# A hybrid decoder layer: the forget gate's logarithm taken straight from the tanh, its complement moved to ACT

## The chip, the cores and the metric

The kernel runs on one core of a Trainium2 chip. The metric is the device time of one execution in microseconds (us). A core has TensorE (PE in the profile, its weight loads PEld), VectorE (DVE), ScalarE (ACT), GpSimd (POOL) and SyncE (SP), whose queue issues the DMA transfers. Each engine works off its own list of instructions in order; engines wait for each other by semaphores. Matmul results land in PSUM banks, everything else lies in SBUF, and what doesn't fit there is parked in DRAM.

## The reference

One layer on 1024 tokens of width 1024: two token mixers side by side, HGRN2 (a gated linear recurrence) and a sparse attention, merged by gates, then a SwiGLU channel mixer. The part that the change touches is the forget gate of the recurrence:

```python
f = lb + (1.0 - lb) * jax.nn.sigmoid(f_logit.astype(f32))
q_h = heads(q, HG_DK)
k_h = heads(1.0 - f, HG_DK)
v_h = heads(i, HG_DV)
b = jnp.cumsum(heads(jnp.log(f), HG_DK), axis=3)
...
q_dec = q_h * jnp.exp(b)
k_inv = k_h * jnp.exp(-b)
k_end = k_h * jnp.exp(b_last - b)
```

There are 8 heads of 128 channels, and the sum runs within chunks of 64 tokens. With t = tanh(f_logit / 2) the gate is f = lbm + lb1 * t, where lb1 = (1 - lb) / 2 and lbm = lb + lb1 are one number per channel.

## The kernel before

The program has four stretches: the first projections and the compressed keys; the middle, where attention units and the recurrence are interleaved; the merge of both mixers and the output projection; the channel mixer.

The middle is built from two streams. An attention unit (function unit, L767) is one group of heads and 128 queries: scores into PSUM (tile sc, two banks, L806), mask, minimum and eviction on DVE (P, L826), exponential on ACT (L828), scaling on POOL (L838), transposes on PE (pt, L845), split into a high part on ACT (ph, L120) and a rest on DVE (pl, L128), and products with the values (pv, L898 and L899). The other stream is filler for PE: projections of the tokens (tile pj, two banks, L145 to L147, 24 matmuls for a group of 128 channels and 512 tokens), among them for each head the forget gate (forget), the query (query), two mixing gates and an output gate. When all heads are done, the filler goes on with the up projection of the recurrence's output (up_a, L957; again pj, now from tiles ab). It reads the output Ad of all 8 heads through a buffer abr (two of them) and splits it into ab (8 tiles, in eight places).

For a head, forget computes t for both halves of the tokens on ACT (L564). Two DVE instructions (L571) turn t into f; they are tied so that the second half goes first. Two logarithms on ACT follow (L576), then for each half 1 - f on DVE (L580) and the running sums (L583, two pieces of 256 tokens). query multiplies by exp(b) (L590, L594), states and outputs use exp(-b) (L615) and the rest on PE (L628 to L664). Tanh, Exp and Ln don't all share one of ACT's function tables, so a table load (ACT_TABLE_LOAD) stands ahead of a logarithm that follows other functions, and another ahead of the next Exp.

The order on each engine is not the order of the code: a scheduler replays the program with its own estimates and orders each engine's list by that, with the priorities that the code sets (tc.high_priority). A few removed or added instructions therefore shift the interleaving of everything behind them. After the last attention unit the merge begins: the attention's output Bd is read through the same two abr buffers into the same eight places of ab, which the last group of up_a gives free, and the tiles p2 (named p in the profile, L953) are built from them, eight steps of 3 matmuls for each group.

Of the kernel before, what the change touches and what calls it, by code (L numbers as in the profile page):

```python
# [9 lines left out]
F32 = mybir.dt.float32  # L10
F32R = mybir.dt.float32r
I32 = mybir.dt.int32
AF = mybir.ActivationFunctionType
OP = mybir.AluOpType
# [9 lines left out]
HH = 8  # L24
# [87 lines left out]
def body(tc, xT, xS, pos, csa, csb, wA, wB, wG, lbl, normg, kpos, kw1, kb1, kw2, kb2, vpos, vw1, vb1,  # L112
         vw2, vb2, wuh, wun, wo, ln1, wfg, wfu, wfd, ln2, out, dbg=None):
    nc = tc.nc
# [34 lines left out]
    with ctx:  # L149
# [44 lines left out]
        def proj_T(ps, w, half, c0=0):  # L194

            h, l = w
            sl = slice(half * 512, half * 512 + 512)
            cc = slice(c0, c0 + 128)
            for k in range(KT):
                mm3(ps, h[:, k, cc], l[:, k, cc], xh[:, k, sl], xl[:, k, sl], k == 0, k == KT - 1)  # L200
# [308 lines left out]
        def single(name, i):  # L509
            return chunk(H["w"], wB[SINGLES[name] + i], 128, "act", "pool", 1)  # L510
# [15 lines left out]
        H = {}  # L526

        def begin_recurrence():
            h1 = H["h1"] = p1h.enter_context(tc.tile_pool(name="h1", bufs=1))
            H["w"] = px.enter_context(tc.tile_pool(name="wpb", bufs=2, side="right"))  # L530

            lb = h1.tile([128, HH], F32, name="lb")
            lb1 = h1.tile([128, HH], F32, name="lb1")
            lbm = h1.tile([128, HH], F32, name="lbm")
            lg = h1.tile([128, 2, HH], F32, name="lg")
            lt = h1.tile([128, 2, HH], F32, name="lt")
            ng = h1.tile([128, 1], F32, name="ng")
            nc.sync.dma_start(lg, lbl)
            nc.sync.dma_start(ng, normg)
            nc.vector.tensor_tensor(lt[:, 0], lg[:, 0], lg[:, 1], op=OP.max)  # L540
            for j in range(2):
                nc.vector.tensor_tensor(lg[:, j], lg[:, j], lt[:, 0], op=OP.subtract)
            nc.scalar.activation(lg, lg, AF.Exp)
            nc.vector.tensor_tensor(lt[:, 0], lg[:, 0], lg[:, 1], op=OP.add)
            nc.vector.reciprocal(lt[:, 1], lt[:, 0])
            nc.vector.tensor_tensor(lb, lg[:, 0], lt[:, 1], op=OP.mult)

            nc.vector.tensor_scalar(lb1, lb, -0.5, 0.5, op0=OP.mult, op1=OP.add)
            nc.vector.tensor_tensor(lbm, lb, lb1, op=OP.add)
            nc.vector.tensor_scalar(ng, ng, 0.5, None, op0=OP.mult)  # L550
            hmi = cs[:, C_HM:C_HM + 128].bitcast(I32)
            at = h1.tile([128, 4, 128], F32, name="at")
            nc.vector.memset(at, 0.0)
            H.update(lb1=lb1, lbm=lbm, ng=ng, hmi=hmi, at=at)

        def forget(h, T):

            h1 = H["h1"]
            W = single("hf", h)
            for half in range(2):  # L560
                p = psp.tile([128, 512], F32, name="pj")
                proj_T(p, W, half)
                f = T["f", half] = h1.tile([128, 512], F32, name="f", bufs=4)
                nc.scalar.activation(f, p, AF.Tanh, scale=0.5)  # L564
                yield

            i = None
            for half in (1, 0):
                f = T["f", half]
                with (tc.issue_after(i.ins) if i is not None else nullcontext()):  # L570
                    i = nc.vector.tensor_scalar(f, f, H["lb1"][:, h:h + 1], H["lbm"][:, h:h + 1],  # L571
                                                op0=OP.mult, op1=OP.add)
            with tc.high_priority(offset=400):
                for half in range(2):
                    b = T["b", half] = h1.tile([128, 512], F32, name="b", bufs=2)
                    nc.scalar.activation(b, T["f", half], AF.Ln)  # L576
            for half in range(2):
                f, b = T["f", half], T["b", half]

                nc.vector.tensor_scalar(f, f, -1.0, 1.0, op0=OP.mult, op1=OP.add)  # L580
                for j in range(2):
                    bj = b[:, 256 * j:256 * j + 256]
                    nc.vector.tensor_tensor_scan(bj, cs[:, C_RS:C_RS + 256], bj, 0.0, op0=OP.mult, op1=OP.add)  # L583
# [113 lines left out]
        def recurrences():  # L697

            Ts = [{} for _ in range(HH)]
            later = {}  # L700

            def at(n, fn, *a):
                later.setdefault(n, []).append((fn, a))

            for h in range(HH):
                T, n = Ts[h], 10 * h
                at(n + 3, begin_states, h, T)
                at(n + 3, states, h, 0, T)
                at(n + 3, outputs, h, 0, T)
                at(n + 6, states, h, 1, T)  # L710
                at(n + 6, outputs, h, 1, T)
                at(n + 10, finish, h, T)
            n = 0
            for h in range(HH):
                T = Ts[h]
                for _ in itertools.chain(forget(h, T), query(h, T), mixing_gate(0, h), output_gate(h, T),
                                         mixing_gate(1, h)):
                    for fn, a in later.pop(n, ()):
                        with tc.high_priority(offset=800):
                            fn(*a)  # L720
                    yield
                    n += 1
            for n in sorted(later):
                for fn, a in later[n]:
                    with tc.high_priority(offset=800):
                        fn(*a)
# [185 lines left out]
        def filler():  # L912

            for i in range(4):
                for _ in recurrence_values(i):
                    yield 5.2
            pi.close()
            pw.close()
            begin_recurrence()
            for _ in recurrences():  # L920
                yield 6.6
            p1h.close()
            px.close()
            begin_up()
            for m in range(KT):
                up_a(m)
                yield 10.4
# [87 lines left out]
        for m in range(KT):  # L1015
            w = chunk(U["wq"], wun[m], 128)
            for half in range(2):
# [11 lines left out]
                                               op0=OP.mult, op1=OP.subtract)  # L1029
# [446 lines left out]
        for n, (P, _, _) in enumerate(order):  # L1476
            ps = down_banks(n) if n else banks
            kept = []
            for j in range(AHEAD if n == 0 else 0, NJ):
                i = n * NJ + j  # L1480
# [92 lines left out]
```

## Time and profile before

| | |
|---|---|
| time, median of 3 runs | 2294.76 us (2293.87 to 2296.46) |
| time of the profiled execution | 2293.27 us |
| its span, first to last instruction | 2291.5 us |
| PE busy | 2226.9 us, 97% |
| DVE busy | 1515.0 us, 66% |
| ACT busy | 1004.9 us, 44% |
| POOL busy | 971.4 us, 42% |

The profile is of one execution. Its time lies 1.77 us over its span, and 1.49 us under the median of the timed runs. Busy PE time counts each matmul to its modelled end, so matmuls in a dense row overlap, and idle time is what is left between them.

### The profile page before, as it was taken

The page shows a single profiled execution, that of the slowest core. Times are in us where ns is not written, and L with a number is a line of the kernel's source. Part 1 is how long each engine was busy: PE and PEld are TensorE (multiplying, and loading weights), DVE is VectorE, ACT ScalarE, POOL GpSimd, SP SyncE. Part 2 cuts the span into 40 slices and gives each one's busy share as a digit, 9 for nine tenths or more (in the row PEclk, how much of TensorE's full clock was granted, in tenths as well). Part 3 has the DMA queues.
Part 4 walks back from the last instruction along what each step waited for, and adds up shares of the span by engine and source line. Part 5 has one row for each costly group of instructions (what it writes and reads, how often), then busy time and mean ns, then how long its engine had stood idle before and what let it go on. Part 6 is the DMA issues. An engine that isn't in the chain of part 4 may idle for free.

```text
span 2291.5 us, 33097 instructions
## 1 busy us (share of the span) xinstructions
PE 2226.9 (97%) x11616; PEld 1884.8 (82%) x11616; DVE 1515.0 (66%) x3644; ACT 1004.9 (44%) x1832; POOL 971.4 (42%) x755
## 2 busy tenths in 40 slices
PE   8999999999999999999999999999999999999995
PEld 6888999788888888888888787878788788888884
DVE  6555157878687777677776964435855664535989
ACT  5321145665565655566555643223432232325441
POOL 0222022444443435444444531212189997740733
PEclk9999999999999999999999999999999999999998
DMA  6544421214111141112310536443444333246552
GB/s 215 167 170 152 129 86 33 72 47 127 54 49 63 51 119 51 57 44 68 104 65 26 176 120 196 148 147 125 147 170 149 122 106 111 97 156 211 180 165 92
DMA packets 146488, 261.62 MB, mean 114 GB/s; under 512 B 15634, under 2 KB 66194, under 8 KB 141202
## 3 DMA queue, kind: packets, MB, share of 16 engines
q1 hardware_dynamic: 146322, 259.50, 34.3%
q8 instruction: 92, 1.51, 0.3%
q14 instruction: 74, 0.61, 0.1%
HBM read 184.21 MB, written 75.24 MB: 113 GB/s over the span
## 4 chain that ended last, share of the span: by engine, by line
PE 82%; DVE 7%; DMA 4%; POOL 3%; issue 2%; ACT 2%; SPq 0%; DVEq 0%; ACTq 0%; POOLq 0%
PE pj L145 8%; PE pj L147 8%; PE pj L146 8%; PE sc L806 5%; PE pt L845 5%; PE pa L1144 4%; PE pc L1144 4%; PE pd L1144 4%; PE pv L898 2%; PE pv L899 2%; PE p L145 2%; PE p L147 2%; PE p L146 2%; PE pb L1144 2%; PE pa L146 2%; PE pa L147 2%
## 5 line engine op out<-in xcount | busy, mean ns | idle before, releaser
L838 POOL TENSOR_TENSOR P<-P,sm 128x640 f32<-128x640 f32 (+6 forms) x192 | 206.6, 1080 | 328.2 <-DVE sm L834 222.9
L828 ACT ACTIVATE P<-P,mx 128x640 f32<-128x640 f32 (+7 forms) x256 | 188.3, 736 | 171.8 <-DVE mx L826 168.0
L146 PE MATMUL pj<-xl,wh 128*128 128x512 f32 x640 | 255.1, 399 | 0.0
L145 PE MATMUL pj<-xh,wh 128*128 128x512 f32 x640 | 255.0, 398 | 0.0
L147 PE MATMUL pj<-xh,wl 128*128 128x512 f32 x640 | 254.9, 399 | 0.0
L120 ACT CAST ph<-pt 128x512 fp32r<-128x512 f32 (+1 forms) x296 | 167.4, 582 | 157.0 <-PE pt L845 138.3
L806 PE MATMUL sc<-K,Q 128*128 128x352 f32 (+8 forms) x800 | 206.1, 344 | 5.4 <-DVE mx L826 5.1
L128 DVE TENSOR_TENSOR pl<-pt,ph 128x512 fp32r<-128x512 f32 x264 | 179.3, 686 | 32.8 <-ACT ph L120 30.5
L845 PE MATMUL pt<-ca,P 128*128 128x128 f32 x1056 | 172.4, 273 | 0.5 <-DVE pl L128 0.3
L845 PEld LDWEIGHTS pt<-ca,P 128*128 128x128 f32 x1056 | 133.7, 141 | 28.3 <-DVE pl L128 0.5
L806 PEld LDWEIGHTS sc<-K,Q 128*128 128x128 f32 x800 | 134.4, 190 | 22.3 <-DVE mx L826 4.3
L128 POOL TENSOR_TENSOR wl<-w,wh 128x1024 fp32r<-128x1024 f32 x48 | 115.2, 2401 | 79.7 <-ACT wh L120 69.8
L826 DVE CUSTOM_DVE_ANT_0 P<-sc,cs 128x352 f32<-128x352 f32 (+5 forms) x192 | 90.0, 477 | 76.3 <-PE sc L806 54.4
L146 PEld LDWEIGHTS pj<-xl,wh 128*128 128x128 f32 x640 | 120.5, 188 | 20.8
L145 PEld LDWEIGHTS pj<-xh,wh 128*128 128x128 f32 x640 | 120.5, 188 | 20.7
L147 PEld LDWEIGHTS pj<-xh,wl 128*128 128x128 f32 x640 | 120.4, 188 | 20.7
L1144 PE MATMUL pa<-B,ac 128*128 128x512 f32 x528 | 131.6, 402 | 4.1 <-DVE u L1222 1.9
L1144 PE MATMUL pc<-T,ac 128*128 128x512 f32 x528 | 130.7, 396 | 2.3 <-DVE u L1175 2.3
L120 ACT CAST wh<-w 128x1024 fp32r<-128x1024 f32 (+2 forms) x75 | 91.3, 1219 | 82.8 <-PE pb L146 37.5
L1144 PEld LDWEIGHTS pa<-B,ac 128*128 128x128 f32 x528 | 101.9, 194 | 28.5 <-DVE u L1222 2.3
L1144 PEld LDWEIGHTS pc<-T,ac 128*128 128x128 f32 x528 | 99.0, 188 | 26.9 <-DVE u L1175 3.2
L120 ACT CAST ac<-su 128x512 fp32r<-128x512 f32 x88 | 53.2, 620 | 137.9 <-POOL su L1302 71.0
(361 smaller groups left out, 5996.3 us busy)
## 6 DMA issues: line engine op xcount, KB each, us to landing
w<-in_wB_dram SPq DMA_DIRECT2D x40, 512.0 KB, 3.3
tr<-Td SPq DMA_DIRECT2D x73, 256.0 KB, 2.7
Td<-tg SPq DMA_DIRECT2D x61, 256.0 KB, 2.0
w<-in_wA_dram SPq DMA_DIRECT2D x12, 1024.0 KB, 6.0
wf<-in_wfg_dram SPq DMA_DIRECT2D x11, 1024.0 KB, 5.1
wf<-in_wfu_dram SPq DMA_DIRECT2D x11, 1024.0 KB, 5.1
b<-in_wfd_dram SPq DMA_DIRECT2D x44, 256.0 KB, 3.0
Qd<-rh SPq DMA_DIRECT2D x32, 256.0 KB, 2.3
```

Source lines behind the costliest of these rows:

```text
L120: nc.scalar.copy(o, i)
L128: e.tensor_tensor(o, a, b, op=OP.subtract)
L145: nc.tensor.matmul(ps, ah, bh, start=start, stop=False)
L146: nc.tensor.matmul(ps, ah, bl, start=False, stop=False)
L147: nc.tensor.matmul(ps, al, bh, start=False, stop=stop)
L806: nc.tensor.matmul(ps[:, :wx], Q[:, g], KV_["k", br][:, c_, ks], start=c_ == 0, stop=c_ == 1)
L826: nc.vector.tensor_tensor_reduce(po, pi_, m, -0.125, mx[:, g, 0:1] if pi else -3.0 * NEG, op0=OP.add, op1=OP.min, accum_out=mx[:, g, pi:pi ...
L828: nc.scalar.activation(P[:, :nk], P[:, :nk], AF.Exp, scale=-1.0, bias=mx[:, g, npc - 1:npc], accum_out=den[:, g:g + 1])
L838: nc.gpsimd.tensor_tensor(P[:, :nk], P[:, :nk], cg.to_broadcast([128, nk]), op=OP.mult)
L845: nc.tensor.transpose(pt[:n, g * 128:g * 128 + 128], src[:, g], ident)
L898: nc.tensor.matmul(pv, v, ph, start=i == 0, stop=False)
L1144: nc.tensor.matmul(ps, A[:, a, k], B[:, b, k], start=begins and k == 0 and n == 0, stop=k == 3 and n == 2, skip_group_check=not begins)
```

## The change

The two DVE instructions that make f are gone. The logarithm reads t itself and gets lb1 and lbm as ACT's scale and offset, one number per partition each. The complement 1 - f is computed by ACT too, as lb2 + lbn * t with lb2 = 1 - lbm and lbn = -lb1, in place over t. Two tiny tiles and two tiny DVE instructions are added once. The tie that put the second half first goes away with the instructions that it tied.

```diff
             nc.vector.tensor_tensor(lbm, lb, lb1, op=OP.add)
+
+            lb2 = h1.tile([128, HH], F32, name="lb2")
+            lbn = h1.tile([128, HH], F32, name="lbn")
+            nc.vector.tensor_scalar(lb2, lbm, -1.0, 1.0, op0=OP.mult, op1=OP.add)
+            nc.vector.tensor_scalar(lbn, lb1, -1.0, None, op0=OP.mult)
...
-            i = None
-            for half in (1, 0):
-                f = T["f", half]
-                with (tc.issue_after(i.ins) if i is not None else nullcontext()):
-                    i = nc.vector.tensor_scalar(f, f, H["lb1"][:, h:h + 1], H["lbm"][:, h:h + 1],
-                                                op0=OP.mult, op1=OP.add)
             with tc.high_priority(offset=400):
                 for half in range(2):
                     b = T["b", half] = h1.tile([128, 512], F32, name="b", bufs=2)
-                    nc.scalar.activation(b, T["f", half], AF.Ln)
+                    nc.scalar.activation(b, T["f", half], AF.Ln, scale=H["lb1"][:, h:h + 1],
+                                         bias=H["lbm"][:, h:h + 1])
             for half in range(2):
                 f, b = T["f", half], T["b", half]
 
-                nc.vector.tensor_scalar(f, f, -1.0, 1.0, op0=OP.mult, op1=OP.add)
+                nc.scalar.activation(f, f, AF.Identity, scale=H["lbn"][:, h:h + 1], bias=H["lb2"][:, h:h + 1])
```

The names that start with lb stand for the small per-channel tiles. On ACT, at the first head, the list before reads as follows (f is t, b the logarithm, P an attention tile):

```order
L564 ACTIVATE f<-pj 128x512
L828 ACTIVATE P_3674,sm<-P_3674,mx 128x640
L907 COPY ob<-pv 64x512
L120 CAST ph<-pt 128x512 x2
L120 CAST wh<-w 128x1024
L564 ACTIVATE f<-pj 128x512
L828 ACTIVATE P_3674,sm<-P_3674,mx 128x640
L576 ACT_TABLE_LOAD
L576 ACTIVATE b<-f 128x512 x2
L615 ACT_TABLE_LOAD
L615 ACTIVATE ki<-b 128x512
L590 ACTIVATE eb<-b 128x512 x2
```

The same place on ACT after the change:

```order
L569 ACTIVATE f<-pj 128x512
L575 ACT_TABLE_LOAD
L575 ACTIVATE b<-f,lbm,lb_4721 128x512
L580 ACTIVATE f<-f,lb_4737,lbn 128x512
L615 ACT_TABLE_LOAD
L615 ACTIVATE ki<-b 128x512
L590 ACTIVATE eb<-b 128x512
...
L569 ACTIVATE f<-pj 128x512
L575 ACT_TABLE_LOAD
L575 ACTIVATE b<-f,lbm,lb_4721 128x512
L580 ACTIVATE f<-f,lb_4737,lbn 128x512
L590 ACT_TABLE_LOAD
```

The two logarithms no longer stand side by side: each follows its own half's tanh, with a table load ahead of it and one behind it. Over the whole program the list of ACT has 35 table loads, and 19 before.

On DVE, at the same head, before (P is the eviction of scores):

```order
L826 ISA P_3674,mx<-sc,mb,mx 128x320
L826 ISA mx 128x1
L571 TENSOR_SCALAR f<-f,lb_4721,lbm 128x512 x2
L832 TENSOR_SCALAR sm<-sm 128x1
L833 RECIPROCAL sm<-sm 128x1
L834 TENSOR_TENSOR sm<-sm,gates 128x1
L580 TENSOR_SCALAR f<-f 128x512
L583 SCALAR_TENSOR_TENSOR b<-cs,b 128x256 x2
L580 TENSOR_SCALAR f<-f 128x512
L583 SCALAR_TENSOR_TENSOR b<-cs,b 128x256 x2
L826 ISA P_3674,mx<-sc,bb 128x320
```

And DVE at the second half of that head, after the change:

```order
L826 ISA P_3674,mx<-sc,bb 128x320
L826 ISA mx 128x1
L832 TENSOR_SCALAR sm<-sm 128x1
L833 RECIPROCAL sm<-sm 128x1
L834 TENSOR_TENSOR sm<-sm,gates 128x1
L583 SCALAR_TENSOR_TENSOR b<-cs,b 128x256 x2
L826 ISA P_3674,mx<-sc,mb,mx 128x320
```

Between two evictions of scores there were eight instructions of the gate, and now there are two running sums for each half.

The third place is on PE, where the last attention unit ends (pv is its output, pj the up projection, ab_14452 the last of its eight input tiles). Before:

```order
L898 MATMUL pv_12531<-ph_12641,V0_10110 128x512
L145 MATMUL pj_14823<-ab_14447,wh_14787 128x512
L146 MATMUL pj_14823<-ab_14447,wh_14787 128x512
L147 MATMUL pj_14823<-ab_14447,wl_14788 128x512
L899 MATMUL pv_12531<-pl_12642,V0_10110 128x512
L145 MATMUL pj_14823<-ab_14452,wh_14787 128x512
L146 MATMUL pj_14823<-ab_14452,wh_14787 128x512
L147 MATMUL pj_14823<-ab_14452,wl_14788 128x512
L145 MATMUL pj_14859<-ab_14417,wh_14853 128x512
```

After (ab_14440 is the last input tile of the up projection, ab_14999 the first tile of the merge):

```order
L145 MATMUL pj_14943<-ab_14440,wh_14907 128x512
L146 MATMUL pj_14943<-ab_14440,wh_14907 128x512
L147 MATMUL pj_14943<-ab_14440,wl_14908 128x512
L898 MATMUL pv_12525<-ph_12635,V0_10108 128x512
L899 MATMUL pv_12525<-pl_12636,V0_10108 128x512
L145 MATMUL p2_15047<-ab_14999,wh_15039 128x512
L146 MATMUL p2_15047<-ab_14999,wh_15039 128x512
```

Before, 99 matmuls of the up projection stood behind the last unit's last product; now none does, and the merge follows at once.

## Rows read from the trace of the kernel before

**Rows 1.** The page: span, and busy time of each engine.

```profile
span 2291.5 us, 33097 instructions
PE 2226.9 (97%) x11616; PEld 1884.8 (82%) x11616; DVE 1515.0 (66%) x3644; ACT 1004.9 (44%) x1832; POOL 971.4 (42%) x755
```

**Rows 2.** Busy time by stretch: length, each engine (instructions), PE clock, DMA share, GB/s.

```profile
420.00:1270.00 850.00, 844.66 (x4797) 726.67 (x4796) 643.24 (x2175) 493.62 (x981) 374.16 (x323) 1.00 0.21 65
1270.00:1296.00 26.00, 20.72 (x130) 17.34 (x128) 23.20 (x73) 19.55 (x35) 16.66 (x11) 0.93 0.72 258
1296.00:1416.00 120.00, 120.00 (x597) 100.02 (x596) 76.83 (x240) 54.01 (x119) 40.42 (x39) 1.00 0.43 139
1416.00:1430.00 14.00, 9.98 (x33) 6.82 (x33) 8.97 (x10) 5.96 (x7) 0.00 (x0) 0.88 0.87 292
```

**Rows 3.** Waits of PE from 420 to 1260 us: total, times, longest.

```profile
PE sc L806 <- DVE mx L826: 3.4, 2, 2.7
PE pv L899 <- DVE pl L128: 0.7, 1, 0.7
PE pv L898 <- ACT ph L120: 0.6, 1, 0.6
```

**Rows 4.** ACT from 420 to 1300 us by group: busy, mean ns, idle before.

```profile
L828 ACT ACTIVATE P<-P,mx 128x512 f32<-128x512 f32 x28 | 20.2, 723 | 11.5 <-DVE mx L826 11.4
...
L576 ACT ACT_TABLE_LOAD x8 | 10.3, 1283 | 0.1
...
L590 ACT ACTIVATE eb<-b 128x512 f32<-128x512 f32 x16 | 9.5, 623 | 0.0
...
L576 ACT ACTIVATE b<-f 128x512 f32<-128x512 f32 x16 | 9.2, 624 | 9.2 <-DVE f L571 9.2
```

**Rows 5.** DVE from 420 to 1300 us by group, the gate's instructions.

```profile
L583 DVE TENSOR_TENSOR_SCAN b<-cs,b 128x256 f32<-128x256 f32 x32 | 27.4, 890 | 0.0
...
L571 DVE TENSOR_SCALAR f<-f,lb,lbm 128x512 f32<-128x512 f32 x16 | 22.2, 1430 | 3.8 <-ACT f L564 3.8
...
L580 DVE TENSOR_SCALAR f<-f 128x512 f32<-128x512 f32 x16 | 7.7, 484 | 0.6 <-ACT b L576 0.4
```

**Rows 6.** DVE in order of time at the first head: start, duration, instruction.

```profile
434.64 2.30 DVE L571 TENSOR_SCALAR f<-f,lb,lbm 128x512 f32<-128x512 f32 x2
...
437.66 1.42 DVE L580 TENSOR_SCALAR f<-f 128x512 f32<-128x512 f32 x1 [0.26 <-ACT b L576]
...
440.50 2.10 DVE L583 TENSOR_TENSOR_SCAN b<-cs,b 128x256 f32<-128x256 f32 x2
442.53 0.46 DVE L826 CUSTOM_DVE_ANT_1 P<-sc,bb 128x320 f32<-128x320 f32 x1
```

**Rows 7.** PE in order of time at the first head.

```profile
443.05 0.56 PE L806 MATMUL sc<-K,Q 128*128 128x320 f32 x2 [2.66 <-DVE mx L826]
```

**Rows 8.** ACT in order of time at the first head.

```profile
435.50 0.19 ACT L828 ACTIVATION_READ_ACCUMULATOR P<-P,mx 128x1 f32 x1
435.70 1.28 ACT L576 ACT_TABLE_LOAD   x1
437.00 1.15 ACT L576 ACTIVATE b<-f 128x512 f32<-128x512 f32 x2
```

**Rows 9.** Chain that ended last, at the merge: start, duration, what.

```profile
1395.35 2.77 DMA Bd<-ob
...
1418.38 5.44 DMA abr<-Bd
...
1423.85 1.05 ACT ab L120
```

**Rows 10.** DVE in order of time, one split of a merge tile.

```profile
1439.59 1.23 DVE L128 TENSOR_TENSOR ab<-abr,ab 128x1024 fp32r<-128x1024 f32 x1 [0.91 <-ACT ab L120]
```

**Rows 11.** PE in order of time, two matmuls of the dense up projection.

```profile
1392.00 0.39 PE L145 MATMUL pj<-ab,wh 128*128 128x512 f32 x1
1392.22 0.39 PE L146 MATMUL pj<-ab,wh 128*128 128x512 f32 x1
```

More of the change, by code (lines that the diff above doesn't have):

```diff
@@ L553, in begin_recurrence @@
             nc.vector.memset(at, 0.0)
-            H.update(lb1=lb1, lbm=lbm, ng=ng, hmi=hmi, at=at)
+            H.update(lb1=lb1, lbm=lbm, lb2=lb2, lbn=lbn, ng=ng, hmi=hmi, at=at)
         def forget(h, T):
```

## The prediction

> **What bounds the kernel now.** I read the page first. PE is busy for 97% of the span, DVE for 66%, ACT for 44% [rows 1], so PE's work is the floor, and only the time in which PE waits can be won. The change touches the middle alone (420 to 1270 us, and through the order of the lists what follows it up to about 1450 us), so I cut that part into stretches next: PE is busy for 844.66 of 850 us from 420 to 1270, for 20.72 of 26 while the recurrence's output is loaded for the up projection, for all of 120 us after that, and for 9.98 of 14 where the merge begins [rows 2]. So the whole of PE's idle time near the change is 5.3 + 5.3 + 4.0 us. DVE is busy for 643 of the 850 us and ACT for 494 (58%) [rows 2]: neither is the bound, but both work their lists in order, and what stands at the head of one holds up the rest.
>
> The waits of PE then say who it is that holds it. From 420 to 1260 us two waits for the eviction of scores on DVE make 3.4 us, and PE waited for a split on ACT once, for 0.6 us [rows 3]. The longer of the two I followed to its place: PE stands still for 2.66 us ahead of a pair of score matmuls at 443.05 us [rows 7], and DVE at that time is in the forget gate of the first head. Its gate work runs from 434.64 us with three tiny instructions among it, and the next eviction of scores begins only at 442.53 us [rows 6]: 7.9 us in which no score bank comes free. The other wait has the same form at the last head.
>
> **DVE's share of the change.** Gone are 16 instructions of L571, 22.2 us, and 16 of L580, 7.7 us [rows 5]: 29.9 us of DVE's 643. The running sums stay, 32 of 0.89 us [rows 5]. They now stand as two pairs for each head with evictions between them, so the longest block of gate work falls from 7.9 us to 2 x 0.89 = 1.8 us, and to 3.1 us if DVE comes to them one table load (1.28 us) too early and has to wait for the logarithm. Both lie well below what PE survived at six of the eight heads. I take both waits as gone, 3.4 us. The bounds are 0 (another instruction is late in the new order) and all of PE's idle time in the stretch, 5.3 us. What is late next after a gate is the query's product, and that hangs on PE's own projection.
>
> **ACT's share.** The list has 35 table loads in place of 19. A load takes 1.283 us [rows 4], so 16 more are 20.5 us. No row shows an Identity of this size with scale and offset from a tile. Between the exponential without such an operand (0.623 us) and the one with an offset from a tile (0.723 us) lies 0.10 us [rows 4]; two such operands make 0.82 us, and 16 complements 13.1 us. The logarithm grows by the same 0.2 us from 0.624, 3.2 us in 16; the lower bound for both operands is no surcharge at all. Together ACT gets 36.8 us more in the stretch and goes from 58% to 62%. Against that, ACT waited 9.2 us at the head of its list for L571 ahead of the logarithms [rows 4], and this wait is gone with the instruction.
>
> What counts is how long ACT lets the others wait. Before, a head held ACT for a load, that wait (9.2 / 8 = 1.15 us), two logarithms (1.15 us together at the first head [rows 8]) and the load back: 4.9 us, eight times. Now a half holds it for a load, 0.82, 0.82 and a load back: 4.2 us, sixteen times, if each half has its own load back. Who is queued behind it is the high part of a transposed tile (L120), for which PE's product with the values (L898) waits, and that is the one wait of 0.6 us in 840 us [rows 3]. So a hold of 4.9 us cost PE nothing that shows. The bounds are 0 and 16 x 1.28 = 20.5 us, all new loads laid bare; I take one load, 1.3 us, near the lower end, since that is what the eight holds before are nearest to.
>
> The Trainium skill, page "ScalarE: Activation LUTs", section "What ACT_TABLE_LOAD costs", speaks against the change: it puts a switch of tables at about 2.66 us, of which 1.28 are the load and 1.38 a drain of the engine. By that the 16 switches would cost ACT 42.6 us, and 22.1 of these would not be in the sum above. The trace doesn't bear the drain out: the load at 435.70 us begins 0.01 us after the instruction ahead of it has ended, and all eight such loads have 0.1 us of idle time ahead of them [rows 4, 8].
>
> **What moves behind it.** The scheduler's new order reaches PE from about 429 us on and ends at about 1452 us, where both lists are the same again. The work on PE is the same, instruction for instruction. Two places could pay or gain.
>
> The first is the start of the up projection. Its input can be loaded only when the last token projection has freed the place, and until then PE has attention work alone: 105 matmuls before, 69 now (both counted in the order). In the trace that stretch has 130 matmuls in 20.72 us of work [rows 2], 0.16 us each, so 36 fewer take away 5.7 us of cover from a chain that costs 5.3 us of idle time already. The splits of those tiles, on the other hand, stand closer together in the new list of ACT. I take 0, with -5.3 and +5.7 us as bounds.
>
> The second is the start of the merge. The 99 matmuls behind the last unit were 99 x 0.23 = 22.8 us of cover (a matmul every 0.22 to 0.23 us [rows 11]); now there are none. What they covered, though, was mostly not needed: from the last product to the merge's tiles 7 and 8 there is the store of 2.77 us, the load of 5.44, the cast of 1.05 [rows 9] and the rest of 1.23 [rows 10], 10.5 us and two short copies, and the first merge matmul that reads tile 7 is the 52nd, 12 us behind. The longer chain is that of the buffers: three pairs of tiles pass through two places, each 5.44 + 1.05 + 1.23 = 7.7 us, 23.2 us. PE's list before came to tile 8 with its 85th merge matmul, 19.6 us, and the shortage of 3.6 us fits the 4.0 us of idle time in that stretch [rows 2]. Now it comes to it with the 62nd, 14.3 us, 5.3 us earlier; but the first splits no longer stand behind those of the output projection's weights, so the chain starts earlier too. The bounds are -4.0 (all of the idle time gone) and +5.3 us; I take the middle, +0.7.
>
> **The sum** on the profiled execution: 2293.27 - 3.4 + 1.3 + 0 + 0.7 = 2291.9 us. That execution lay 1.5 us under the median of the timed runs, so for a median I forecast 2293.4 us. A measurement of this kernel tells about 0.2% from no change, 4.6 us: below 2290.2 is faster, above 2299.4 slower. My case is no change that can be told, 0.45, with 2290 to 2299 as its own range.
>
> **Rivals.** The first is slower: the table loads reach PE. The sixteen loads sit right behind a tanh, among casts for which PE waits, and at the first head ACT now also stands waiting for DVE's sums before it goes on to casts. If half of the loads end on PE's path, 8 x 1.28 = 10.3 in place of 1.3 gives 2302.4 us; it decides from six bare loads on (7.7 us). For it speaks that the scheduler's estimates and the chip need not agree; against it that ACT has 38% of its time left and that PE waited 0.6 us for it in all. 0.17.
>
> The second is slower too: both chains of loads come out at their upper ends, 5.7 and 5.3 in place of 0 and 0.7, 2303.7 us. For it speaks the lost cover of 99 matmuls, against it that the buffers and not the last unit set the pace there. 0.10.
>
> The third is faster: with 30 us less on DVE, which is busy for 23.20 of 26 us [rows 2] where the up projection's tiles are split, the waits in the stretch go entirely (5.3) and one of the two chains gives its idle time back (4.0): 2294.76 - 5.3 - 4.0 = 2285.5 us. For it speaks that DVE is the releaser of the most waits in rows 3; against it that no gate work is left at either chain, so DVE is not lighter just there. 0.28.
>
> That the change does not do what it says is in my own case: DVE's 30 us are off PE's path at six of eight heads.
>
> **Range and chances.** From the third rival to the second, 2285 to 2304 us, which leaves out about 2 in 10. Faster 0.28, same 0.45, slower 0.17 + 0.10 = 0.27.
>
> **What would show it.** L571 gone and L580 on ACT at about 0.8 us; 16 loads ahead of the logarithms, at 1.28 us each and without a drain; no wait of PE for an eviction of scores at a gate; PE's waits for L120 on ACT still about 1 us from 420 to 1260 us. The prediction is wrong if these waits grow past 7 us, or if PE's idle time at one of the two chains of loads differs from 5.3 or 4.0 us by more than 5.

## The result and the profile after

The changed kernel takes 2310.19 us (median of 6 runs, 2307.23 to 2311.22), the kernel before beside it 2294.23 (6 runs, 2293.26 to 2296.46): a ratio of 1.007, with a 95% interval of 1.006 to 1.0079. It is slower by some 16 us, and 6 us above the range that I gave. The page of after, to be read beside [rows 1]:

```profile
span 2308.8 us, 33045 instructions
PE 2233.4 (97%) x11616; PEld 1890.0 (82%) x11616; DVE 1498.3 (65%) x3614; ACT 1043.7 (45%) x1864; POOL 972.3 (42%) x755
```

The span is 17.3 us longer. ACT gained 38.8 us of work, about as announced (36.8). DVE lost 16.7 us and not the 29.9 of the two instructions that are gone; what took up the other 13 us was not followed. PE has the same 11,616 matmuls. Where PE fell behind is read best from the number of matmuls that it has begun by a given time. The view of busy time from the start up to three times, first of before, then of after (length, busy time and instructions of PE, PEld, DVE, ACT and POOL, then PE's clock, DMA share, GB/s):

```profile
0.00:1220.00 1220.00, 1202.91 (x7002) 1050.10 (x7003) 838.56 (x2542) 623.97 (x1171) 444.62 (x373) 1.00 0.29 91
0.00:1313.00 1313.00, 1290.63 (x7503) 1125.22 (x7504) 912.33 (x2773) 679.30 (x1273) 491.43 (x407) 1.00 0.29 92
0.00:1414.00 1414.00, 1391.63 (x8002) 1209.48 (x8003) 973.05 (x2969) 721.00 (x1368) 519.42 (x436) 1.00 0.30 95
```

```profile
0.00:1220.00 1220.00, 1197.44 (x6923) 1044.17 (x6924) 812.33 (x2455) 651.05 (x1181) 440.15 (x367) 0.99 0.29 91
0.00:1313.00 1313.00, 1283.48 (x7410) 1118.31 (x7411) 878.87 (x2657) 701.55 (x1271) 479.80 (x396) 0.99 0.28 90
0.00:1414.00 1414.00, 1382.89 (x7907) 1200.63 (x7908) 944.12 (x2886) 748.14 (x1373) 517.35 (x431) 0.99 0.29 93
```

By 1220 us, when the gates of all heads are through, after is 79 matmuls behind. Counted the other way, its matmul number 7000 (the first is number 0) starts at 1233.5 us and that of before at 1219.7: 13.8 us lost, of which 0.8 lie ahead of the first gate and the rest among the gates. Number 7500 is 20.6 us late, so another 7 went at the start of the up projection, and at the end of the program the delay is 17.3 us: the merge gave some 3 us back.

The waits of PE from 420 to 1260 us in after (total, times, longest), against [rows 3]:

```profile
PE sc L806 <- DVE mx L826: 4.5, 3, 1.8
PE sc L806 <- DVE sm L833: 2.5, 1, 2.5
PE pv L898 <- ACT ph L120: 1.5, 2, 0.8
PE pv L899 <- DVE pl L128: 1.0, 1, 1.0
```

The waits for DVE before score matmuls should have gone. They doubled, from 3.4 to 7.0 us. ACT's groups and DVE's running sums in after, same stretch (busy, mean ns of one, idle before and who ended it), against [rows 4, 5]:

```profile
L575 ACT ACT_TABLE_LOAD x16 | 20.5, 1283 | 0.3
L575 ACT ACTIVATE b<-f,lbm,lb 128x512 f32<-128x512 f32 x16 | 13.1, 816 | 0.2
L580 ACT ACTIVATE f<-f,lb,lbn 128x512 f32<-128x512 f32 x16 | 13.0, 814 | 0.4
...
L583 DVE TENSOR_TENSOR_SCAN b<-cs,b 128x256 f32<-128x256 f32 x32 | 24.3, 798 | 9.2 <-ACT b L575 9.2
```

The prices were right: 0.82 us for the logarithm and for the complement, 1.283 for a load, and 16 loads ahead of the logarithms where there were 8 (8 more are loads back). New is the last figure: DVE stood still for 9.2 us at the head of its list, waiting for the logarithm, where before it never waited at this line.

How a load gets through to PE is seen at the third head. ACT of after in order of time (start, duration):

```profile
639.41 1.28 ACT L575 ACT_TABLE_LOAD   x1
640.71 0.81 ACT L575 ACTIVATE b<-f,lbm,lb 128x512 f32<-128x512 f32 x1
641.54 1.28 ACT L828 ACT_TABLE_LOAD   x1
642.84 1.04 ACT L828 ACTIVATE P<-P,mx 128x896 f32<-128x896 f32 x1
```

DVE of after at the same time, idle time before an instruction in brackets:

```profile
641.56 1.27 DVE L583 TENSOR_TENSOR_SCAN b<-cs,b 128x256 f32<-128x256 f32 x2 [1.06 <-ACT b L575]
...
644.00 0.15 DVE L832 TENSOR_SCALAR sm<-sm 128x1 f32<-128x1 f32 x1 [1.12 <-ACT P L828]
...
644.21 0.51 DVE L826 CUSTOM_DVE_ANT_0 P<-sc,cs,mx 128x288 f32<-128x288 f32 x1
```

And PE of after:

```profile
641.83 0.49 PE L845 MATMUL pt<-ca,P 128*128 128x128 f32 x3
644.87 1.51 PE L806 MATMUL sc<-K,Q 128*128 128x352 f32 x4 [2.55 <-DVE sm L833]
```

The first load holds DVE for 1.06 us at the running sum, the load back holds it for 1.12 us at a tiny instruction that waits for the exponential, and the eviction that frees the score bank (644.21) stands behind both in DVE's list. PE stood for 2.55 us. After it the clock is low, in the view of busy time of after by stretch:

```profile
642.00:645.00 3.00, 0.45 (x4) 0.24 (x2) 1.88 (x9) 2.99 (x5) 2.02 (x2) 0.96 0.00 0
645.00:648.00 3.00, 3.00 (x13) 2.73 (x13) 2.94 (x8) 3.00 (x7) 1.67 (x2) 0.50 0.00 0
648.00:651.00 3.00, 3.00 (x15) 2.51 (x14) 2.75 (x9) 1.27 (x3) 2.63 (x3) 0.97 0.02 5
```

PE is busy for 0.45 us of the first 3, and in the next 3 its granted clock is 0.50, the lower of its two levels, while it is busy throughout. So a stall here costs more than its own length, and the idle time of PE does not show all of it. Two more places among the gates of after are like it: the granted clock is 0.72 from 432 to 438 us, behind a wait of PE of 1.84 us, and 0.76 from 857 to 864 us, behind one of 0.95. The three together make some 10 us at the lower level. At the first, a projection matmul starts every 0.43 us, against 0.22 to 0.23 before and after it, so about half of the 10 us, 5 us, is lost to PE (an estimate from these numbers). In the kernel before the clock is 1.00 from 420 to 1255 us.

### The profile page after: what moved, and what is told of

Same layout as the page of the kernel before. It is cut to its first block, busy times and chain, and to the rows that moved or that the text cites. A ratio compares the mean times of both kernels' runs of the same rounds, so it can differ in the third digit from the quotient of the medians.

```text
span 2308.8 us, 33045 instructions
## 1 busy us (share of the span) xinstructions
PE 2233.4 (97%) x11616; PEld 1890.0 (82%) x11616; DVE 1498.3 (65%) x3614; ACT 1043.7 (45%) x1864; POOL 972.3 (42%) x755
## 4 chain that ended last, share of the span: by engine, by line
PE 80%; DVE 7%; DMA 5%; POOL 3%; ACT 2%; issue 2%; SPq 0%; DVEq 0%; ACTq 0%; POOLq 0%
PE pj L145 8%; PE pj L146 8%; PE pj L147 8%; PE sc L806 5%; PE pt L845 5%; PE pa L1144 4%; PE pc L1144 3%; PE pd L1144 3%; PE pv L898 2%; PE pv L899 2%; PE p L145 2%; PE p L146 2%; PE p L147 2%; PE pa L145 2%; PE pa L146 2%
## 5 line engine op out<-in xcount | busy, mean ns | idle before, releaser
L120 ACT CAST wh<-w 128x1024 fp32r<-128x1024 f32 (+2 forms) x75 | 91.5, 1220 | 78.7 <-PE pb L146 36.7
```

Source lines behind the costliest of these rows:

```text
L120: nc.scalar.copy(o, i)
```

## The experiments

The theory after the result was the prediction's first rival: the loads reach PE. The others were that the new order of the lists is at fault (the second rival), and that ACT's complement is. Where an expectation numbers its theories, the numbers hold for that text. All kernels in one table; loads are ACT's table loads, and idle time of PE is the length of the stretch less its busy time, in the profiled execution:

| kernel | loads | median us | ratio to before, 95% | idle 420:1255 | 1255:1330 | 1400:1480 |
|---|---|---|---|---|---|---|
| before | 19 | 2294.2 to 2294.8 | | 5.3 | 5.3 | 4.7 |
| after | 35 | 2310.19 | 1.006 to 1.0079 | 11.1 | 8.6 | 3.6 |
| tied | 21 | 2287.64 | 0.9961 to 0.9981 | 3.7 | 4.3 | 1.5 |
| before_untied | 35 | 2306.44 | 1.0034 to 1.0072 | 7.9 | 9.0 | 4.4 |
| dvecomp | 35 | 2306.01 | 1.0037 to 1.0067 | 11.5 | 5.2 | 2.8 |
| tied_dvecomp | 21 | 2298.81 | 1.001 to 1.0028 | 5.5 | 8.9 | 3.7 |
| tied_twice | 37 | 2297.52 | 1.0001 to 1.002 | 8.9 | 3.5 | 2.0 |
| before_twice | 35 | 2309.92 | 1.0052 to 1.0086 | 11.9 | 8.9 | 2.2 |
| before_actcomp | 19 | 2307.33 | 1.004 to 1.007 | 5.4 | 6.3 | 9.3 |
| after_tanh | 3 | 2299.9 | 1.0013 to 1.0032 | 5.6 | 9.2 | 3.4 |
| before_tanh | 3 | 2301.54 | 1.0021 to 1.0046 | 9.6 | 4.7 | 3.8 |
| tied_linear | 3 | 2284.15 | 0.9942 to 0.9967 | 1.0 | 4.2 | 2.3 |
| tied_again | 21 | 2287.63 | 0.9959 to 0.9981 | 3.9 | 4.6 | 1.7 |
| after_halves | 35 | 2311.24 | 1.0059 to 1.0085 | 11.0 | 6.5 | 4.3 |
| tied_halves | 21 | 2288.23 | 0.9961 to 0.998 | 3.8 | 4.6 | 3.2 |

**tied.** The tie that the change dropped comes back on ACT: both logarithms stand behind the second half's tanh, in a row.

```diff
-                nc.scalar.activation(f, p, AF.Tanh, scale=0.5)
+                last = nc.scalar.activation(f, p, AF.Tanh, scale=0.5)
...
-                    nc.scalar.activation(b, T["f", half], AF.Ln, scale=H["lb1"][:, h:h + 1],
-                                         bias=H["lbm"][:, h:h + 1])
+                    with tc.issue_after(last.ins):
+                        last = nc.scalar.activation(b, T["f", half], AF.Ln, scale=H["lb1"][:, h:h + 1],
+                                                    bias=H["lbm"][:, h:h + 1])
```

> The changed kernel, but with the first logarithm tied behind the second half's tanh, so that both logarithms of a head stand side by side: 21 table loads in the list in place of 35, everything else of the change kept. Theory of the loads (the second pair of table loads per head holds ACT, DVE's sums and maxima wait for it, and PE waits behind these): about 12 us of the 16 come back, 2294 to 2300 us, and PE's idle time from 420 to 1255 us falls by more than half. Theory of the complement (0.82 us more on ACT for each half is what hurts): nothing comes back, 2306 to 2312 us. Theory of the order (any new interleaving costs about as much): no better than the changed kernel on average, 2300 to 2312 us.

It is faster than both kernels: 22.5 us under after, 7 under before. Its waits of PE from 420 to 1260 us:

```profile
PE pv L899 <- ACT ph L120: 1.2, 2, 1.0
PE pv L906 <- DVE ph L128: 1.1, 1, 1.1
PE sc L807 <- DVE mx L827: 0.6, 1, 0.6
```

The waits for evictions of scores are down to 0.6 us. DVE itself, though, waits for the logarithms at its running sums for 11.6 us in tied, longer than the 9.2 of after: such a wait is not by itself a wait of PE. The tie also changes the order of everything behind it, so the 22.5 us are not the loads' alone.

**before_untied, dvecomp, tied_dvecomp.** The first takes the tie out of the kernel before; the others leave the complement on DVE, without and with the tie.

```diff
-            for half in (1, 0):
+            for half in range(2):
                 f = T["f", half]
-                with (tc.issue_after(i.ins) if i is not None else nullcontext()):
-                    i = nc.vector.tensor_scalar(f, f, H["lb1"][:, h:h + 1], H["lbm"][:, h:h + 1],
-                                                op0=OP.mult, op1=OP.add)
+                nc.vector.tensor_scalar(f, f, H["lb1"][:, h:h + 1], H["lbm"][:, h:h + 1],
+                                        op0=OP.mult, op1=OP.add)
```

```diff
-                nc.scalar.activation(f, f, AF.Identity, scale=H["lbn"][:, h:h + 1], bias=H["lb2"][:, h:h + 1])
+                nc.vector.tensor_scalar(f, f, H["lbn"][:, h:h + 1], H["lb2"][:, h:h + 1],
+                                        op0=OP.mult, op1=OP.add)
```

> The kernel before without the tie: f and 1 - f stay on DVE, but each half's logarithm may follow its own half, and the list has 35 table loads in place of 19. Theory of the loads: slower than before by about 12 us, 2302 to 2310 us, though nothing was moved to ACT. Theory of the complement: as before, 2292 to 2297 us. Theory of the order: anywhere from 2292 to 2310 us.

> The changed kernel with the complement back on DVE (one multiply-add with the two tiles), the logarithm straight from the tanh, not tied: 35 loads. Theory of the loads: still slow, 2303 to 2312 us. Theory of the complement: 2292 to 2299 us. Theory of the order: anywhere from 2295 to 2312 us.

> Both at once: logarithms straight from the tanh and side by side, complement on DVE; 21 loads, DVE 22 us lighter than before, ACT as before but for 0.2 us in each logarithm. Theory of the loads: 2290 to 2297 us, as fast as the kernel before or a little faster. Theory of the complement: the same. Theory of the order: anywhere from 2290 to 2312 us.

The old code without its tie loses 11.7 us, with nothing moved to ACT: what the tie was worth, in loads and in order together, is nearly three quarters of what the change lost. Without the complement on ACT, after is only 4 us faster, and its idle time among the gates is the same 11.5 us. With the tie, the complement on ACT is 11.2 us the better place, but by matmul number 7000 tied_dvecomp is only 2.9 us behind tied. Most of the rest comes at the start of the up projection (4.3 against 8.9 us idle) and at the start of the merge (1.5 against 3.7), where no complement is left; that is order.

**tied_twice and before_twice.** These add loads, and little else: one logarithm of a single column for each head, right behind the first half's tanh, its result unused.

```diff
+                if half == 0:
+                    with tc.issue_after(last.ins):
+                        nc.scalar.activation(H["dm"], f[:, 0:1], AF.Ln, scale=H["lb1"][:, h:h + 1],
+                                             bias=H["lbm"][:, h:h + 1])
```

> The suspected cost by itself: the run called tied plus, for each head, one logarithm of a single column right behind the first half's tanh, whose result nobody uses. It brings a second pair of table loads per head (37 loads in the list, 21 in tied) and leaves the order of PE's list as it was but for 436 of 11156 places, the gate's work undivided. Theory of the loads: slower than tied by 8 to 14 us, 2296 to 2302 us. Rival (what hurts in the changed kernel is that the gate is done in two pieces and the exponentials in two places, not the loads): as tied within 3 us, 2285 to 2291 us.

> The same added logarithm in the kernel before: 35 loads in place of 19. Theory of the loads: slower than before by 8 to 14 us, 2302 to 2309 us. Rival: as before, 2292 to 2297 us.

tied_twice is the cleaner of the two, since PE's list differs from that of tied in 436 of 11,156 places: 16 more loads cost 9.9 us, and PE's idle time among the gates goes from 3.7 to 8.9 us. There too the clock falls behind waits of PE (3.15 and 0.79 us): it is 0.83 from 660 to 670 us and 0.79 from 968 to 976, and 1.00 throughout in tied. In before_twice the loads and the new order together make 15.4 us; 2,816 of the trace's 11,616 matmuls stand elsewhere than in before (counted the same way, 489 in tied_twice).

**before_actcomp.** Only the complement goes to ACT, in the kernel before; no load is added.

```diff
-                nc.vector.tensor_scalar(f, f, -1.0, 1.0, op0=OP.mult, op1=OP.add)
+                nc.scalar.activation(f, f, AF.Copy, scale=-1.0, bias=1.0)
```

> One part of the change alone: the kernel before with only the complement 1 - f moved to ACT (a copy with scale -1 and offset 1); f stays on DVE, the logarithms stay side by side, 19 loads. If the complement on ACT is worth something by itself, as the 11 us between tied and tied_dvecomp would have it: 2284 to 2291 us. If that difference is the order's alone: 2292 to 2298 us. Theory of the complement as a cost: over 2300 us.

A miss: 2307.33 us, 12.8 over the kernel before. The view by stretch of this kernel, at the gates, at the start of the up projection and at the start of the merge:

```profile
420.00:1255.00 835.00, 829.61 (x4699) 712.50 (x4698) 627.27 (x2099) 496.14 (x978) 370.39 (x317) 1.00 0.22 66
1255.00:1330.00 75.00, 68.73 (x363) 58.94 (x362) 58.22 (x158) 38.81 (x67) 37.72 (x25) 0.91 0.51 170
...
1400.00:1480.00 80.00, 70.69 (x319) 57.08 (x317) 46.16 (x106) 33.18 (x62) 14.19 (x15) 0.94 0.54 173
```

Among the gates it is nearly as good as before (5.4 us idle, 2.7 us behind at matmul number 7000). It loses at the two places behind, 6.3 and 9.3 us idle at a clock of 0.91 and 0.94, where the last attention unit now ends behind the up projection, between it and the merge, with waits of 4.5 and 2.6 us for its probabilities. At matmul number 8125, in the merge, it is 10.4 us behind; the other 5 us of the profiled execution come later and were not followed. So an order alone, with no load and no gate work at that place, moved the time by some 8 us, half of what the whole change cost; comparisons in which it moves say nothing about loads.

**after_tanh, before_tanh, tied_linear, tied_again.** To hold the order and take the loads away, the logarithm is replaced by a function that needs no load. So after_tanh, before_tanh and tied_linear leave the logarithm out and do not compute the layer; they are there for the time alone. In the first, for instance:

```diff
+            lbg = h1.tile([128, HH], F32, name="lbg")
+            nc.vector.tensor_scalar(lbg, lbm, -1.0, None, op0=OP.add)
...
-                    nc.scalar.activation(b, T["f", half], AF.Ln, scale=H["lb1"][:, h:h + 1],
-                                         bias=H["lbm"][:, h:h + 1])
+                    nc.scalar.activation(b, T["f", half], AF.Tanh, scale=H["lb1"][:, h:h + 1],
+                                         bias=H["lbg"][:, h:h + 1])
```

> The changed kernel with the logarithm left out: in its place stands a tanh of the gate less one (scale lb1, offset lbm - 1), of the same size and operands, whose table is the one already loaded. 32 of the 35 table loads are gone; the lists of PE (but for 4 of 11,156 places), POOL and SP are those of the changed kernel. So it is the new order without the loads. Loads cost the 12 us or so (theory 1): about 2298 us, 2295 to 2301, PE's idle time from 420 to 1255 us down from 11.1 to 4 us or less, and the idle time at the start of the up projection (8.5 us) as it was. Loads cost all of the loss, that at the up projection too (theory 2): 2291 to 2294. The new order is at fault and the loads are hidden (theory 3): 2306 to 2311, idle time as it was.

> The kernel before with the logarithm left out in the same way (a tanh of the negated gate): 16 of 19 table loads are gone and the lists of PE, DVE, POOL and SP are those of the kernel before, place for place. The prediction took eight holds of 4.9 us as free. If they are (theory 1 and 3): 2293 to 2296 us, PE's idle time from 420 to 1255 us 4.5 us or more. If each load costs PE wherever it stands (theory 2 carried over, 12 us for 16 more loads): 2283 to 2288. In between, the price for each load rises with their number.

> The tied kernel with the logarithm left out (its first-order term, an Identity with the same scale and an offset less one): 3 table loads in place of 21, PE's list the same but for 4 places. If the loads at one place for each head are free: 2286 to 2289 us, as tied. If they cost 0.5 us each, 18 of them: 2278 to 2281.

> The changed kernel with both logarithms tied behind the second half's tanh once more (21 loads), to have it beside the three others: 2286 to 2289 us, 0.2 to 0.4% under the kernel before, by theory 1 and 2. Theory 3 has no number for it but the earlier 2287.6.

after_tanh settles the first question. With the lists of after and 32 loads less it takes 2299.9 us, 10.3 under after. Its busy time by stretch, and from the start to the three times used above:

```profile
0.00:1220.00 1220.00, 1202.22 (x6982) 1049.16 (x6983) 817.43 (x2478) 615.99 (x1161) 444.68 (x370) 1.00 0.29 91
0.00:1313.00 1313.00, 1286.06 (x7448) 1120.01 (x7449) 888.74 (x2690) 665.69 (x1248) 485.51 (x399) 0.99 0.29 91
0.00:1414.00 1414.00, 1387.06 (x7960) 1204.55 (x7960) 954.49 (x2922) 712.32 (x1354) 520.89 (x435) 0.99 0.30 94
...
1255.00:1330.00 75.00, 65.84 (x349) 54.42 (x348) 57.62 (x167) 40.13 (x71) 33.98 (x24) 0.91 0.47 160
```

By 1220 us it is 20 matmuls behind the kernel before (after: 79), by 1313 us it is 55 behind. So the loads' 10 us all lie among the gates, and the loss at the start of the up projection is there without them: 9.2 us of idle time, 8.6 in after. Among the gates the idle time fell to 5.6 us, not to 4 as expected; 3.5 us of it is still PE waiting for evictions of scores.

The third head shows how the loads got through: with the same lists and no load, DVE waits neither at the running sums nor at the tiny instruction, and PE waits for 0.19 us where it stood for 2.55. Over 420 to 1260 us DVE's waits for exponentials fall from 56.0 to 45.1 us, and those at the running sums from 9.2 to nothing. The 10.3 us can be nearly added up: 5.5 us of idle time of PE (11.1 less 5.6), and the 5 us or so of the lower clock, which is 1.00 among the gates here.

before_tanh missed under every theory: the same lists as before, 16 loads less, and 7 us slower. The traces show why ACT's time isn't all. POOL of before at the second head, and DVE:

```profile
550.51 1.07 POOL L618 TENSOR_TENSOR ke<-b 128x512 f32<-128x512 f32 x1 [4.85 <-DVE b L583]
552.66 1.29 POOL L622 TENSOR_TENSOR ki<-ki,f 128x512 f32<-128x512 f32 x1 [1.08 <-ACT ki L615]
```

```profile
550.60 2.12 DVE L583 TENSOR_TENSOR_SCAN b<-cs,b 128x256 f32<-128x256 f32 x2
```

The same place in before_tanh:

```profile
552.76 1.07 POOL L618 TENSOR_TENSOR ke<-b 128x512 f32<-128x512 f32 x1 [4.85 <-DVE b L583]
553.79 1.67 POOL L622 TENSOR_TENSOR ki<-ki,f 128x512 f32<-128x512 f32 x1
```

```profile
552.85 3.16 DVE L583 TENSOR_TENSOR_SCAN b<-cs,b 128x256 f32<-128x256 f32 x2
```

Two running sums take 1.3 us when POOL is idle (1.27 in the third head of after, above), 2.12 when one POOL product lies beside them, and 3.16 when two follow each other. In before, the load back on ACT delays ki, and with it POOL's second product, until the sums are done. Without the load the two products come back to back. Over 32 sums DVE's time goes from 27.4 to 34.7 us. That these 7.3 us are the 7 us of the kernel was not tested apart.

tied_linear has the same lengthening (35.8 us for the sums, tied 24.3) and still gains 3.5 us over tied: 18 loads at one place for each head cost 0.2 us each or somewhat more. tied_again repeats tied to 0.01 us in the median.

**after_halves and tied_halves.** What remained was the start of the up projection. There PE's longest wait in after is for a rest on DVE:

```profile
1298.46 1.11 PE L845 MATMUL pt<-ca,P 128*128 128x128 f32 x4 [4.53 <-DVE pl L128]
```

DVE of after ahead of it, and POOL:

```profile
1293.26 2.28 DVE L883 TENSOR_TENSOR_SCAN im<-im 128x16 f32<-128x16 f32 x1
1295.58 2.24 DVE L884 TENSOR_SCALAR im<-im,t 128x16 f32<-128x16 f32 x1
1297.73 0.68 DVE L128 TENSOR_TENSOR pl<-pt,ph 128x512 fp32r<-128x512 f32 x1
```

```profile
1293.14 2.35 POOL L128 TENSOR_TENSOR wl<-w,wh 128x1024 fp32r<-128x1024 f32 x1
1295.44 2.34 POOL L128 TENSOR_TENSOR ab<-abr,ab 128x1024 fp32r<-128x1024 f32 x1
```

Two instructions of 16 columns, about 0.2 us each elsewhere, last as long as the POOL instruction beside them, and end when it ends. The runs cut these POOL instructions in two:

```diff
+        if eng == "pool2":
+            m = o.shape[1] // 2
+            for c in (slice(0, m), slice(m, 2 * m)):
+                nc.gpsimd.tensor_tensor(o[:, c], a[:, c], b[:, c], op=OP.subtract)
+            return
```

> The changed kernel, with POOL's rests of the up projection's weights and inputs (L128, 128x1024, about 2.3 us each) cut into two pieces; 12 more POOL instructions, 443 of 11,156 places of PE's list differ. In the changed kernel two tiny DVE instructions at the start of the up projection (0.18 us elsewhere) took 2.28 and 2.24 us while such a rest ran on POOL, and PE then stood for 4.53 us. Theory 1 (a DVE instruction that reads two operands from SBUF waits for the whole POOL instruction): with pieces of half the length each hold is at most 1.2 us, the wait of 4.5 us falls to 2.5 or less, PE's idle time from 1255 to 1330 us from 8.5 to 4 to 6.5 us, and the time to 2304 to 2308 us. Theory 2 (the wait is the chain of loads, POOL only happened to be busy): the wait and the idle time stay, 2308 to 2312 us.

> The tied kernel with the same cut; 289 places of PE's list differ. Its start of the up projection has 4.3 to 4.6 us of idle time and no wait of this form. By theory 1 there is little to win: 2285 to 2288 us; by theory 2 also none, 2287 to 2289. If 12 more POOL instructions cost something by themselves it shows here: over 2289.

The same two instructions on DVE in after_halves:

```profile
1292.88 1.21 DVE L888 TENSOR_TENSOR_SCAN im<-im 128x16 f32<-128x16 f32 x1
1294.12 1.18 DVE L889 TENSOR_SCALAR im<-im,t 128x16 f32<-128x16 f32 x1
```

And its longest wait of PE from 1255 to 1330 us:

```profile
PE pt L850 <- DVE pl L133: 2.4, 1, 2.4
```

The holds are halved, the wait goes from 4.5 to 2.4 us, and the stretch's idle time from 8.6 to 6.5: the mechanism is as theory 1 said. The time is not: 2311.24 us, no gain. The profiled execution was itself 3.2 us over that median; in it, matmul 8000 starts 2.5 us earlier than in after, but number 8050, at the start of the merge, only 0.3 earlier, and number 8500 0.4 us later. So the gain was gone again some 120 us further on (the excess of this execution comes later, from 1650 us on). tied_halves falls behind at the same place, from 1.1 us ahead of tied to 1.2 behind. Why the start of the merge gave the gain back was not settled. The control shows next to no cost of the cut in all (2288.23 against 2287.6 us).

The Trainium skill, page "SBUF — State Buffer", section "SBUF: two separate sides", says that a DVE instruction with two SBUF inputs and a GpSimd instruction that reads SBUF exclude each other for a whole instruction. The trace agrees for the first of the two, which reads two operands from SBUF: 2.28 us beside POOL's 2.35, and 1.21 when that is halved. The second was held likewise (2.24 us beside 2.34, then 1.18), but it is a TENSOR_SCALAR that reads one tile and one number per partition, so that sentence alone does not cover it.

## Why the prediction was wrong

**The step that failed is ACT's share: "I take one load, 1.3 us, near the lower end".** The 16 loads more cost 9.9 us in tied_twice; in the new lists all 32 of the gates cost 10.3 us (after less after_tanh), and the share of the 16 that before has too could not be had apart, since before_tanh brought POOL in. The figure of the first rival, 8 bare loads or 10.3 us, was met, and I gave it 0.17; that it was met so closely is luck, since that rival had casts in mind and no clock. The inference behind the small value was that a hold of ACT of 4.9 us had cost PE nothing at eight heads. It looked at one way only, from ACT's casts to the product with the values; those waits did grow little, from 0.6 to 1.5 us, though after_tanh has none of them. The larger part of the idle time came by DVE (7.0 us of waits for evictions, 3.7 in after_tanh), which waits in its list for the logarithm, and then for an exponential behind the load back, while the evictions of scores stand behind it (third head, above). In the kernel before, the list of DVE held its own work on the gate at that place, and the running sums never waited [rows 5]. The prediction did name a wait of one load at the sums, but set it against the length of the old block and not against what ACT does next. What a stall takes from PE's clock was not in the sum at all, and by the estimate above it was about half of the loads' price. Neither of the two signs that I had set for being wrong came up: PE's waits for casts stayed far under 7 us, and its idle time at the two chains moved by 3.3 and 1.1 us, not by 5. Of the things to be seen, only the absence of waits for evictions failed.

**DVE's share, 3.4 us won, was in place but not in this order.** tied has the 3.4 us nearly whole (0.6 us left), with the same work on DVE. In after_tanh, with the loads out of the way, the waits for evictions are again 3.5 us. So the lower bound, nothing, came about.

**The start of the up projection, 0 with -5.3 and +5.7 as bounds, cost about 7 us.** The estimate by lost cover stood at the upper bound and was nearer than the middle that I took. It also had the wrong place: PE's longest wait there, 4.5 of the 8.6 us, was for tiny DVE instructions held by POOL's long ones, on which no term of the sum rested, and with less attention work between (the matmuls from the last token projection to the first of the up projection are 124 before and 84 after, counted in the traces). Its idle time grew by only 3.3 us; the clock, 0.91 from 1255 to 1330 us in after and 0.98 in before, took a part of the rest. How the 7 us divide was not settled.

**The start of the merge, +0.7 with -4.0 and +5.3, gave back about 3 us**: a mis-sized term inside its bounds. Its idle time fell from 4.7 to 3.6 us.

**The rivals were not exclusive.** The first rival's 9.0 us over my sum and the 5.7 us of the second's first part together make 2293.4 + 9.0 + 5.7 = 2308.1 us, against 2310.19 measured. The range went only as far as one of them alone.

The sentence on the drain holds: in after, the load at 641.54 us begins as the logarithm (640.71 + 0.81) ends, to 0.02 us, so the price of a switch on ACT is its 1.283 us. By the 2.66 us that the Trainium skill, page "ScalarE: Activation LUTs", section "What ACT_TABLE_LOAD costs", gives, 16 switches would have made an estimated 42.6 us. The trace does not agree: the view of groups has 0.3 us of idle time ahead of the 16 loads at the logarithms.

## What to carry to other kernels

When a change lets two instructions drift apart that shared a table load, follow what waits for each of them in the other engines' in-order lists; in this kernel the added load was paid where the next reader stands, although ACT had room. An ordering tie that goes away with the code it was attached to is part of the change: put it back on the new producer and compare (here 22 us, loads and order together). And before judging an edit by its time in a scheduled kernel, make a twin with the same lists and without the suspected cost, since the order alone moved this kernel by some 8 us.

## What was unexpected of the hardware

A DVE instruction of 16 columns lasted 2.28 us beside a POOL instruction of 128x1024, and 1.21 us when that was cut in two; a running sum lasted about 0.66 us alone and up to 1.71 beside one (before_tanh). Taking 16 table loads, with the logarithms, out of the kernel before made it 7 us slower. And PE's granted clock was 0.50 and 0.53 over 14 us at the start of the up projection, in after:

```profile
1290.00:1297.00 7.00, 3.05 (x11) 1.90 (x10) 6.40 (x13) 4.90 (x7) 7.00 (x5) 0.50 0.40 149
1297.00:1304.00 7.00, 5.54 (x18) 4.77 (x19) 5.29 (x11) 0.20 (x1) 3.70 (x3) 0.53 0.40 115
```
